# mLSTM values of all heads in 512-column projections, output gates channel-major, output projection in halves of 512

## The chip, the cores and the metric

The kernel runs on one core of a Trainium2 chip. The metric is device time in microseconds (us) for one execution: the median of 3 runs. Engines are named as in the profile: PE is TensorE (matmuls), DVE is VectorE, ACT is ScalarE, POOL is GpSimd, SP issues most of the transfers.

## The reference, cut to what matters

One block of a generator: a normalized and modulated input goes through one wide input projection into three branches (mLSTM, differential attention, state-space scan), which are merged under gates, projected, and followed by a gated conv FFN. There are 512 latent tokens and 256 context tokens, all in float32, D = 1024. The change touches the mLSTM's values `u[1]` (v) and output gates (`o_pre`), and the output projection `w_o`:

```python
u = jnp.split(h @ w_in[l], split_pts, axis=-1)          # u[0:4]: q and k, v, o gate, i and f gates of 4 heads of 128
...
def mlstm_out(h, o_pre, norm_g):
    h = rmsnorm(h.transpose(0, 2, 1, 3), norm_g.reshape(M_HEADS, M_HEAD_DIM)).reshape(bsz, t, M_WIDTH)
    return (jax.nn.sigmoid(o_pre.astype(jnp.float32)) * h).astype(o_pre.dtype)
...
def gated_merge(y_m, y_a, y_s, gate_pre, w_m, w_a, w_s, w_o):
    g_m, g_a, g_s = jnp.split(jax.nn.sigmoid(gate_pre), N_BRANCH, axis=-1)
    return (g_m * (y_m @ w_m) + g_a * (y_a @ w_a) + g_s * (y_s @ w_s)) @ w_o
...
x = x + mod[2][:, None] * gated_merge(...)              # then the second norm and the FFN
```

## The kernel before, in words

Every large product is made of three matmuls on split operands: each float32 weight and activation is kept as a high part (`wh`, `hl0` and the like) and a low part (`wl`, `hl1`), and high x high, high x low and low x high are added up in PSUM. All matmuls of projections are issued by the helper `mm` (L82), so in the profile most of PE's time has that line. A weight piece of 512 KB (`wpiece`, L180) is loaded by SP into one of 2 buffers `wr`, rounded by ACT to `wh` (L176), and DVE, or for every third piece POOL, makes `wl` (L85).

Projections come in two forms. Channel-major (`proj_cm`, L207, and `proj_w`): the weights are stationary, the tokens move, 512 latent tokens at a time (24 matmuls of 512 columns for 128 channels). Token-major (`proj_tm`, L404): 128 tokens are stationary and 256 columns of weights (`wblk`, L194: two pieces) move, 24 matmuls of 256 columns for each token tile. The values of the mLSTM are token-major, for two heads at a time and 6 token tiles (2 of context, 4 latent); so are the output gates of two heads (4 latent tiles), and the output projection in 4 blocks of 256 columns.

The order of the program is written as generators. `run(main, n_main, fill, n_fill)` (L150) spreads the chunks of a filling generator between the chunks of a main one: `m_proj(0)` (projections for heads 0 and 1) with the gate rows; then `m_core(0)` (the recurrence of those heads, small matmuls with much work on DVE and ACT between) filled with `m_proj(1)`; then `m_core(1)` filled with the first projections of the state-space branch (`s_proj(0)`), and so on. The framework then schedules this program: it sets the order on each engine once, by its own costs, and that order is fixed at run time. PSUM has 8 banks: 4 for projections (`pl`, handed out in turn by `psl`) and 4 for everything short-lived (`psx`, by `pss`). A projection can start only when the bank's earlier tile has been read by ACT and DVE. Convolution taps of q, k and of the state-space inputs read their bank once on ACT and twice on DVE (`conv_b`, L478, three taps).

The names that the prediction uses: `kw` are scaled keys, from the keys that are transposed and copied at L660 and L661; `to_cm` (L468) transposes a head's result (L472) and splits it to high and low; `xn` is the input of the second norm, transposed at L1128; the gate rows are a chain of small operations on DVE, ACT and POOL that makes the input and forget gates, ending in a matmul at 64x384.

Of the kernel before, what the change touches and what calls it, by code (L numbers as in the profile page):

```python
# [38 lines left out]
def build(tc, a, out):  # L39
# [13 lines left out]
    def open_ps(nps, nsc):  # L53
        """the pool of short-lived PSUM banks: nps single ones and nsc double ones"""
        if ps_pool:
            ps_pool.pop().close()
        st = ExitStack()
        ps_pool.append(st)
        st.tl = st.enter_context(pool("ps", nps, PSUM)) if nps else None
        st.sc = st.enter_context(pool("sc", nsc, PSUM)) if nsc else None  # L60
# [3 lines left out]
    # banks of one tag are handed out in program order, so a filling stream can have its own  # L64
# [59 lines left out]
    def rstd(o, ssq, n, inv):  # L124
        """1 / sqrt(ssq * inv + EPS) by Newton steps from an exponent-halving start"""
        rsn[0] += 1
        tg = "rs%d" % (rsn[0] % 3)
        x = cst.tile([P, 80], F32, tag=tg, name=tg, bufs=1)
        x, t = x[:, 0:n], x[:, 40:40 + n]
        ts(V, x, ssq, inv, EPS, ALU.mult, ALU.add)  # L130
        ts(V, o.bitcast(I32), x.bitcast(I32), -0.5, 1597463007.0, ALU.mult, ALU.add)
        ts(V, x, x, -0.5)
        for _ in range(3):
            tt(V, t, x, o, ALU.mult)
            tt(V, t, t, o, ALU.mult)
            stt(o, t, 1.5, o, ALU.add, ALU.mult)
# [6 lines left out]
    ssq2 = cst.tile([P, 4, 4], F32, name="ssq2")  # L143
# [6 lines left out]
    def run(main, n_main=1, fill=(), n_fill=0, hp=0, lanes=False):  # L150
        """emit main, with the chunks of fill spread evenly between its chunks"""
# [28 lines left out]
    def wpiece(w, k0, nk, c0, nc_):  # L180
        """rows [k0*P, (k0+nk)*P), columns [c0, c0+nc_) as hi and lo parts [P, nk, nc_]"""
        r = wp.tile([P, 1024], F32, tag="wr", name="wr", bufs=2).rearrange("p (k c) -> p k c", c=nc_)
        lo = wp.tile([P, 1024], F32R, tag="wl", name="wl", bufs=4).rearrange("p (k c) -> p k c", c=nc_)
        nc.sync.dma_start(r, w.rearrange("(k p) c -> p k c", p=P)[:, k0:k0 + nk, c0:c0 + nc_])
        hi = wp.tile([P, 1024], F32R, tag="wh", name="wh", bufs=4).rearrange("p (k c) -> p k c", c=nc_)
        split(hi, lo, r)
        return hi, lo
# [43 lines left out]
    def mod_bc(m, dst, mul=1.0):  # L231
        """rows m, broadcast over the partitions, times mul"""
# [7 lines left out]
    with pool("ph0", 1) as p0:  # L240
        # rows: c, c_ctx, norm1_g, norm2_g
# [68 lines left out]
        # rows of per-gate constants: bias, a_log, sign, dt row mask, ln of the key scale  # L310
# [22 lines left out]
        def h_part(n):  # L333
            """shift and scale of the channels of part n, and h there"""
# [32 lines left out]
        def early(n):  # L367
            """part n of the first projections"""
# [35 lines left out]
    def proj_tm(w, t):  # L404
# [7 lines left out]
        return pl[:, 0:256]  # L412

# [8 lines left out]
    def pcol(which, r):  # L422
        return PT[:, which, r:r + 1]
# [35 lines left out]
    def junk(n):  # L459
        return up.tile([P, 256], mybir.dt.bfloat16, tag="jk", name="jk", bufs=2)[:, 0:n]  # L460
# [7 lines left out]
    def to_cm(y, col):  # L468
        """token-major [P, 4, P] -> channel-major hi/lo [P, T], scaled by col"""
# [3 lines left out]
        hi, lo = ytile()  # L473
        act(hi, tp, AF.Identity, scale=col)
# [139 lines left out]
    def m_proj(hq, st):  # L614
        st["q"], st["k"], st["v"] = [], [], []

        def vals():
            for _ in range(2 - len(st["v"])):
                v = v3(t3(), 130)
                G.memset(v[:, :, 128:130], 1.0)  # L620
                st["v"].append(v)

        if hq == 0:
            vals()
# [15 lines left out]
        w = wblk(w_in, C_VM + hq * 256)  # L640
        vals()
        for t in range(6):
            pt = proj_tm(w, t)
            for hh in range(2):
                S.copy(st["v"][hh][:, t, 0:P], pt[:, hh * P:(hh + 1) * P])  # L645
            if t % 2:
                yield

    def m_core(hq, st, ys):
# [67 lines left out]
        w = wblk(w_in, C_OM + hq * 256)  # L717
        for j in range(4):
            so = xw()
            act(so, proj_tm(w, 2 + j), AF.Tanh, scale=0.5)  # L720
            for hh in range(2):
                ho = hb[hh][:, j, :]
                ts(V, ho, ho, sq[:, hh * 4 + j:hh * 4 + j + 1])
                stt(ho, so[:, hh * P:(hh + 1) * P], 1.0, ho, ALU.add, ALU.mult)
        for hh in range(2):
            ys.append(to_cm(hb[hh], pcol(2, R3_MN + 2 * hq + hh)))
        yield

# [162 lines left out]
    def a_keys(st):  # L891
        """keys of both heads as [hi;lo] along the contraction"""
# [19 lines left out]
    def a_core(p, st, of):  # L912
        so = sm(8)

        def queries(hh, j):
            """[hi;hi] and [lo;lo] of both sub-heads"""
# [101 lines left out]
    def weave(g_, h_, n):  # L1018
        """n chunks of h_ after each of g_"""
# [11 lines left out]
    def mods(s, rt, at, then):  # L1031
        """one modulation section for c: weighted rows summed on the way in, over the partitions at the end"""
# [35 lines left out]
    NP_M, NB_M, NP_S, NB_S, NR = 7, 15, 5, 11, 13  # L1068
    run(m_proj(0, m0), NP_M, gate_rows(), NR)
    run(m_core(0, m0, ym), NB_M, m_proj(1, m1), NP_M)  # L1070
# [63 lines left out]
    wo = {}  # L1134
    for blk, js in ((0, (0, 1, 2, 3)), (1, (0, 1, 2, 3)), (2, (0, 1)), (3, (0, 1)), (2, (2, 3)), (3, (2, 3))):
        if blk not in wo:
            wo[blk] = wblk(a["w_out"][0], blk * 256)
        w = wo[blk]
        for j in js:
            ps = pss()  # L1140
            for k in range(NK):
                hi, lo = w[k // 4]
                for n, (zt, wt) in enumerate(((zh_, hi), (zh_, lo), (zl_, hi))):
                    mm(ps[:, 0:256], zt[k][:, j * P:(j + 1) * P], wt[:, k % 4, :], k == 0 and n == 0, k == NK - 1 and n == 2)
            t_ = xw()
            xc = x1[j][blk // 2][:, (blk % 2) * 256:(blk % 2 + 1) * 256]
            tt(V, t_, ps[:, 0:256], mb[:, blk * 256:(blk + 1) * 256], ALU.mult)
            tt(V, xc, xc, t_, ALU.add)
            act(junk(256), xc, AF.Square, accum=ssq2[:, j, blk:blk + 1])
        if blk == 2 and js[0] == 2:  # L1150
            with tc.high_priority(1000):
                norm2(0, lambda: t2()[:, 0:256])
# [64 lines left out]
    for half in range(2):  # L1217
        # the last token tile is finished in column halves
# [60 lines left out]
```

## Time and profile before

| | |
|---|---|
| median of 3 runs | 1130.47 us (1129.69 to 1135.66) |
| the profiled execution: span from first to last instruction | 1133.3 us |
| mean granted clock of PE, share of full speed | 0.986 |
| PE busy | 1088.3 us, 96% |
| DVE, ACT, POOL busy | 721.9, 477.6, 285.3 us (64%, 42%, 25%) |
| chain that ended last, by engine | PE 80%, DVE 9%, DMA 3%, ACT 3%, POOL 2% |

The profiled execution is one more than the three that are timed, and the page gives its span alone. A span of 1133.3 us with 1088.3 busy on one engine leaves 45 us in which that engine did nothing. The chain that ended last is followed back from the last instruction, at each step to what released it.

### The profile page before, as it was taken

What the parts mean: (1) busy time and instruction counts of PE and PEld (TensorE: products, weight loads), DVE (VectorE), ACT (ScalarE), POOL (GpSimd) and SP (SyncE); (2) the same over time, 40 slices, a digit from 0 to 9 for tenths busy, and PEclk for the clock granted to TensorE, in tenths of its full rate; (3) what the DMA queues carried; (4) which work ended last, traced back from release to release, by engine and by line L of the source; (5) the groups of instructions that cost most, each with busy time, mean ns of one, the idle gap of its engine ahead of it and who ended that gap; (6) DMA issues with size and microseconds to landing.
All of it is one profiled execution on the core that took longest, in us unless ns stands there. A gap on an engine that the chain in (4) does not pass through costs nothing.

```text
span 1133.3 us, 16687 instructions
## 1 busy us (share of the span) xinstructions
PE 1088.3 (96%) x6438; PEld 949.7 (84%) x6438; DVE 721.9 (64%) x1354; ACT 477.6 (42%) x891; POOL 285.3 (25%) x243
## 2 busy tenths in 40 slices
PE   4998999999999998999999999988999999999998
PEld 3597999988888997889998887988888888888887
DVE  6578677768645568886685567677867656651211
ACT  5455454557324233334654573333543443431110
POOL 3230001026423533551061002243212212111110
PEclk9898999999999998999999999999999999999999
DMA  8621212223334337331113202425533333333421
GB/s 297 232 59 56 71 40 57 57 70 94 112 109 117 119 108 230 91 109 54 38 38 81 74 33 79 144 63 159 152 112 93 93 100 91 107 93 93 130 93 38
DMA packets 136416, 113.00 MB, mean 100 GB/s; under 512 B 6609, under 2 KB 115512, under 8 KB 136336
## 3 DMA queue, kind: packets, MB, share of 16 engines
q1 hardware_dynamic: 135712, 111.59, 32.8%
q8 instruction: 51, 0.84, 0.3%
q0 software_dynamic: 624, 0.33, 0.2%
q14 instruction: 29, 0.24, 0.1%
HBM read 109.81 MB, written 2.10 MB: 99 GB/s over the span
## 4 chain that ended last, share of the span: by engine, by line
PE 80%; DVE 9%; DMA 3%; issue 3%; ACT 3%; POOL 2%; SPq 0%; DVEq 0%; ACTq 0%; POOLq 0%
PE pl L82 56%; PE psx L82 19%; DVE t L85 2%; PE sc L82 2%; DMA wr<-in_w_in_dram 1%; ACT t L104 1%; DVE wl L85 1%; DVE t L88 1%; DMA wm<-in_w_mod_dram 1%; PE pl L949 1%; POOL t L85 1%; ACT wh L176 1%; POOL wl L85 1%; DMA t<-in_w_mod_dram 0%; PE psx L276 0%
## 5 line engine op out<-in xcount | busy, mean ns | idle before, releaser
L85 POOL TENSOR_TENSOR wl<-wr,wh 128x1024 fp32r<-128x1024 f32 x59 | 144.5, 2450 | 629.9 <-ACT wh L176 563.4
L176 ACT CAST wh<-wr 128x1024 fp32r<-128x1024 f32 x150 | 157.9, 1053 | 292.9 <-PE pl L82 179.5
L82 PE MATMUL pl<-h,wh 128*128 128x512 f32 (+1 forms) x768 | 223.2, 375 | 4.5 <-DVE ft L88 3.0
L85 DVE TENSOR_TENSOR wl<-wr,wh 128x1024 fp32r<-128x1024 f32 x91 | 119.2, 1312 | 146.8 <-ACT wh L176 144.6
L82 PE MATMUL pl<-hl,wh 128*128 128x512 f32 x608 | 200.4, 397 | 0.6 <-ACT t L758 0.4
L82 PEld LDWEIGHTS pl<-h,wh 128*128 128x128 f32 x768 | 141.0, 189 | 31.0 <-issue 4.1
L82 PE MATMUL pl<-wh,hl 128*128 128x256 f32 x768 | 151.7, 291 | 3.2 <-ACT t L645 3.2
L82 PE MATMUL pl<-h,wl 128*128 128x512 f32 (+1 forms) x384 | 143.0, 374 | 0.0
L82 PEld LDWEIGHTS pl<-hl,wh 128*128 128x128 f32 x608 | 113.0, 189 | 24.5 <-issue 2.0
L82 PEld LDWEIGHTS pl<-wh,hl 128*128 128x128 f32 x768 | 125.2, 196 | 4.1 <-ACT t L645 3.4
L82 PE MATMUL pl<-hl,wl 128*128 128x512 f32 x304 | 120.7, 397 | 0.0
L82 PE MATMUL pl<-wl,hl 128*128 128x256 f32 x384 | 111.3, 290 | 0.0
L82 PEld LDWEIGHTS pl<-h,wl 128*128 128x128 f32 x384 | 72.6, 189 | 12.8
L82 PEld LDWEIGHTS pl<-wl,hl 128*128 128x128 f32 x384 | 75.2, 196 | 0.5
L88 DVE SCALAR_TENSOR_TENSOR ft<-pl,PT,ft 128x511 f32<-128x511 f32 x88 | 65.2, 744 | 6.1 <-ACT ft L104 4.8
L82 PEld LDWEIGHTS pl<-hl,wl 128*128 128x128 f32 x304 | 57.3, 188 | 11.4
L82 PE MATMUL psx<-wl,ah 128*128 128x512 f32 (+1 forms) x176 | 66.2, 376 | 0.0
L82 PE MATMUL psx<-wh,al 128*128 128x512 f32 (+1 forms) x176 | 66.1, 376 | 0.0
L82 PE MATMUL psx<-wh,ah 128*128 128x512 f32 (+1 forms) x176 | 66.0, 376 | 0.0
L85 DVE TENSOR_TENSOR al<-ft,ah 128x512 fp32r<-128x512 f32 x22 | 45.4, 2063 | 31.0 <-ACT ah L176 31.0
L82 PE MATMUL pl<-y,wh 128*128 128x512 f32 x192 | 61.8, 402 | 0.4 <-ACT y L104 0.3
L104 ACT ACTIVATE t<-t 128x512 f32<-128x512 f32 (+4 forms) x55 | 36.9, 684 | 35.7 <-DVE t L88 34.2
(315 smaller groups left out, 2032.2 us busy)
## 6 DMA issues: line engine op xcount, KB each, us to landing
wr<-in_w_in_dram SPq DMA_DIRECT2D x64, 512.0 KB, 4.1
wr<-in_w_up_dram SPq DMA_DIRECT2D x44, 512.0 KB, 3.8
t<-in_w_mod_dram SPq DMA_DIRECT2D x48, 256.0 KB, 4.3
wr<-in_w_down_dram SPq DMA_DIRECT2D x22, 512.0 KB, 3.7
wm<-in_w_mod_dram SPq DMA_DIRECT2D x16, 512.0 KB, 8.1
wr<-in_w_out_dram SPq DMA_DIRECT2D x8, 512.0 KB, 3.4
fc<-in_w_mod_dram SPq DMA_DIRECT2D x16, 256.0 KB, 3.0
xs<-in_x_dram SPq DMA_DIRECT2D x2, 1024.0 KB
```

The costliest lines, as they stand in the source:

```text
L82: return PE.matmul(o, l, r, start=start, stop=stop)
L85: eng.tensor_tensor(out=o, in0=x, in1=y, op=op)
L88: V.scalar_tensor_tensor(out=o, in0=x, scalar=sc, in1=y, op0=op0, op1=op1)
L104: return S.activation(o, x, f, **kw)
L176: S.copy(hi, src)
L949: PE.transpose(out=tp[:, t * P:(t + 1) * P], in_=p0[:, (t0 + t) * P:(t0 + t + 1) * P], identity=ident)
```

## The change

**Values.** `tm_wide` projects the values of all four heads in one go, in `m_proj(0)`. It holds 4 pieces of 2 k-blocks x 512 columns, opens three token tiles at once, each a whole bank of 512 columns, and runs the pieces as the outer loop: 144 matmuls of 512 columns in place of 288 of 256. The values go to four buffers of the `y` tag, which are free until the first branch is finished, and no longer to `t3` tiles; four memsets for their last two columns stand at the beginning. `m_proj(1)` has only q and k of its two heads left, so that the filling of `m_core(0)` is 4 chunks, and `m_proj(0)` counts 12.

**Gates.** In `m_core` the output gates of each head are projected channel-major, 24 matmuls of 512 columns, and the product with (gate + 1) moves behind the transposes, into `to_cm`, where DVE reads the transposed result from PSUM. The scaling of the rows becomes one operation of 128x512 for each head.

**Output projection.** Two halves of 512 columns with pieces of 2 k-blocks; half 0 takes all four token tiles at once, with the pieces as the outer loop; half 1 takes tiles 0 and 1, then 2 and 3. 192 matmuls of 512 in place of 384 of 256. The second norm of tiles 0 and 1 is emitted after the second piece of the last group.

```diff
+    def tm_wide(c0, tiles, sink, n=3):
+        ws = [wpiece(w_in, 2 * i, 2, c0, 512) for i in range(4)]
+        for g0 in range(0, len(tiles), n):
+            grp = [(t, psl()) for t in tiles[g0:g0 + n]]
+            for i, (hi, lo) in enumerate(ws):
+                for t, pl in grp:
...
+                    for kk in range(2):
+                        k = 2 * i + kk
+                        for m, (wt, v) in enumerate(((hi, 0), (lo, 0), (hi, 1))):
+                            mm(pl, h_[v][:, k, tsl], wt[:, kk, :], k == 0 and m == 0, k == NK - 1 and m == 2)
+                    if i == 3:
+                        sink(t, pl)
+                yield
...
-    def to_cm(y, col):
+    def to_cm(y, col, gate=None):
...
         hi, lo = ytile()
+        if gate is not None:
+            stt(gate, gate, 1.0, tp, ALU.add, ALU.mult)
+            tp = gate
         act(hi, tp, AF.Identity, scale=col)
...
+    mv = [v3(ybuf().bitcast(F32), 130, 780) for _ in range(4)]
...
-        w = wblk(w_in, C_VM + hq * 256)
-        vals()
-        for t in range(6):
-            pt = proj_tm(w, t)
-            for hh in range(2):
-                S.copy(st["v"][hh][:, t, 0:P], pt[:, hh * P:(hh + 1) * P])
-            if t % 2:
-                yield
+        else:
+            def sink(t, pl):
+                for h in range(4):
+                    S.copy(mv[h][:, t, 0:P], pl[:, h * P:(h + 1) * P])
+
+            yield from tm_wide(C_VM, range(6), sink)
...
         rstd(sq, sq, 8, 1.0 / P)
-        w = wblk(w_in, C_OM + hq * 256)
-        for j in range(4):
-            so = xw()
-            act(so, proj_tm(w, 2 + j), AF.Tanh, scale=0.5)
-            for hh in range(2):
-                ho = hb[hh][:, j, :]
-                ts(V, ho, ho, sq[:, hh * 4 + j:hh * 4 + j + 1])
-                stt(ho, so[:, hh * P:(hh + 1) * P], 1.0, ho, ALU.add, ALU.mult)
+        so = []
         for hh in range(2):
-            ys.append(to_cm(hb[hh], pcol(2, R3_MN + 2 * hq + hh)))
+            pl, _ = proj_cm(wcol(C_OM + (2 * hq + hh) * P))
+            so.append(t2())
+            act(so[hh], pl, AF.Tanh, scale=0.5)
+            tt(V, hb[hh], hb[hh], sq[:, hh * 4:hh * 4 + 4].unsqueeze(2).broadcast_to([P, 4, P]), ALU.mult)
+        for hh in range(2):
+            ys.append(to_cm(hb[hh], pcol(2, R3_MN + 2 * hq + hh), so[hh]))
...
-    NP_M, NB_M, NP_S, NB_S, NR = 7, 15, 5, 11, 13
+    NP_M, NB_M, NP_S, NB_S, NR = 12, 15, 5, 11, 13
-    run(m_core(0, m0, ym), NB_M, m_proj(1, m1), NP_M)
+    run(m_core(0, m0, ym), NB_M, m_proj(1, m1), 4)
...
-    for blk, js in ((0, (0, 1, 2, 3)), (1, (0, 1, 2, 3)), (2, (0, 1)), (3, (0, 1)), (2, (2, 3)), (3, (2, 3))):
...
+    for half in range(2):
+        ws = [wpiece(a["w_out"][0], 2 * i, 2, half * 512, 512) for i in range(4)]
+        for js in (((0, 1, 2, 3),), ((0, 1), (2, 3)))[half]:
+            grp = [(j, pss()) for j in js]
+            for i, (hi, lo) in enumerate(ws):
+                for j, ps in grp:
+                    for kk in range(2):
...
+                            mm(ps, zt[k][:, j * P:(j + 1) * P], wt[:, kk, :], k == 0 and n == 0, k == NK - 1 and n == 2)
+                if js == (2, 3) and i == 1:
+                    with tc.high_priority(1000):
+                        norm2(0, lambda: t2()[:, 0:256])
```

The order on ACT at the value projection of `m_proj(0)`, before; `pl_803` and `pl_830` are the banks of the first two value tiles, `pl_717` and `pl_718` those of the keys of head 1, and `t_702` is the logarithm of the gate rows:

```order
L645 COPY t_662<-pl_803 128x128 [waits PE_49]
L645 COPY t_664<-pl_803 128x128
L104 ACT_TABLE_LOAD [waits DVE_49]
L104 ACTIVATE t_702<-t_671 64x768 [waits Activation_49]
L104 ACTIVATE t_767<-pl_718,PT 128x256
L104 ACTIVATE t_767<-pl_717,PT 128x512
L645 COPY t_662<-pl_830 128x128 [waits PE_49]
L645 COPY t_664<-pl_830 128x128
```

The same place in the order of the change; `pl_712` and `pl_713` are the keys' banks, `pl_796` and `pl_797` the first two value tiles, `t_769` the logarithm:

```order
L104 ACTIVATE t_762<-pl_713,PT 128x256 [waits PE_49]
L104 ACTIVATE t_762<-pl_712,PT 128x512
L104 ACT_TABLE_LOAD
L104 ACTIVATE t_769<-t_675 64x768 [waits DVE_49]
L659 COPY y<-pl_796 128x128 [waits PE_49]
L659 COPY y<-pl_796 128x128 x3
L659 COPY y<-pl_797 128x128 [waits PE_49]
L659 COPY y<-pl_797 128x128 x3
```

The taps of the keys have moved ahead of the table load and the logarithm, and each value tile has four copies in place of two.

The order on PE at the turn from the first mLSTM core to the second, before; the transposes at L660 are those of the next head's keys, `pl_1915` the last tile of the first X projection of the state-space branch, `pl_2048` and `pl_2049` the second:

```order
L660 MATMUL psx<-ident,t_1188 128x128 [waits PE_49]
L660 MATMUL psx<-ident,t_1188 128x128
L82 MATMUL pl_1915<-hct,wh 128x256
L82 MATMUL pl_1914<-hl_104,wl 128x512
L82 MATMUL pl_1915<-hct,wl 128x256
L82 MATMUL pl_2048<-hl_104,wh 128x512 [waits Activation_49]
L82 MATMUL pl_2049<-hct,wh 128x256 [waits Activation_49]
L82 MATMUL pl_2048<-hl_105,wh 128x512
L82 MATMUL pl_2049<-hct,wh 128x256
```

The same place in the change; L489 are the transposes in `to_cm`, L674 those of the keys, `kw` the first matmuls of the next core, and `pl_1984` the third projection of the state-space branch:

```order
L489 MATMUL psx<-ident,t_1036 128x128 [waits DVE_49,PE_49]
L489 MATMUL psx<-ident,t_1036 128x128 x3
L674 MATMUL psx<-ident,t_1234 128x128 x4
L674 MATMUL psx<-ident,t_1234 128x128 [waits PE_49]
L674 MATMUL psx<-ident,t_1234 128x128
L82 MATMUL psx<-y,kw 128x130 [waits DVE_49,PE_49] x2
L82 MATMUL psx<-y,kw 128x130 [waits DVE_49,Activation_49]
L82 MATMUL psx<-y,kw 128x130 [waits DVE_49]
L82 MATMUL psx<-y,kw 128x130 [waits DVE_49,Activation_49]
L82 MATMUL pl_1984<-hct,wh 128x256 [waits DVE_49]
```

Both X projections, which stood on both sides of the turn, now stand ahead of it; between the transposes and `pl_1984` only the `kw` matmuls are left.

## Rows read from the trace of the kernel before

**Rows 1.** the page's table: engine, busy us (share of the span), instructions
```profile
PE 1088.3 (96%) x6438; PEld 949.7 (84%) x6438; DVE 721.9 (64%) x1354; ACT 477.6 (42%) x891; POOL 285.3 (25%) x243
```

**Rows 2.** windows of PE: start:end, length, busy (matmuls), granted clock, DMA share, GB/s
```profile
380.00:390.00 10.00, 10.00 (x85) 1.00 0.00 0
715.00:735.00 20.00, 20.00 (x172) 1.00 0.35 96
850.00:900.00 50.00, 50.00 (x222) 1.00 0.33 95
```

**Rows 3.** chain that ended last, 80 to 112 us: start, length, what
```profile
85.44 1.28 ACT L104
86.73 0.84 ACT t L104
87.60 1.23 ACT t L104 x2
88.83 0.33 ACT t L645 x2
89.21 19.18 PE pl L82 x109
```

**Rows 4.** timeline of DVE: start, length, line, operation, out<-in, count [idle before]
```profile
102.92 2.35 DVE L85 TENSOR_TENSOR wl<-wr,wh 128x1024 fp32r<-128x1024 f32 x2
105.19 0.55 DVE L85 TENSOR_TENSOR t<-ident,sm 64x384 f32<-64x384 f32 x1
```

**Rows 5.** timeline of PE, the first matmul behind the gate rows' chain
```profile
108.32 0.91 PE L82 MATMUL psx<-t,on 64*128 64x384 f32 x2
```

**Rows 6.** windows of PE: stretches with waits, and what follows them
```profile
85.00:89.00 4.00, 1.04 (x9) 0.88 0.38 111
89.00:95.00 6.00, 5.79 (x27) 0.51 0.01 3
593.00:596.00 3.00, 0.81 (x8) 1.00 0.00 0
596.00:600.00 4.00, 4.00 (x23) 0.58 0.00 0
672.00:675.00 3.00, 1.99 (x17) 1.00 0.01 3
750.00:758.00 8.00, 4.95 (x37) 1.00 0.46 131
```

**Rows 7.** all waits of PE in 108:262, for what: us, times, longest
```profile
PE pl L82 <- DVE t L88: 0.5, 1, 0.5
```

**Rows 8.** timeline of PE at the turn to the second mLSTM core
```profile
183.69 0.60 PE L660 MATMUL psx<-ident,t 128*128 128x128 f32 x4
189.46 1.06 PE L82 MATMUL psx<-t,kw 128*128 128x130 f32 x8
```

**Rows 9.** timeline of ACT at the same turn
```profile
183.78 1.27 ACT L104 ACTIVATE y<-psx,PT 128x512 fp32r<-128x512 f32 x2 [3.05 <-PE psx L472]
184.94 0.86 ACT L661 COPY t<-psx 128x512 f32<-128x512 f32 x2
```

**Rows 10.** timeline of DVE at the same turn
```profile
184.50 1.41 DVE L88 SCALAR_TENSOR_TENSOR y<-psx,PT,y 128x512 fp32r<-128x512 f32 x2 [2.97 <-ACT y L104]
185.83 0.87 DVE L92 TENSOR_SCALAR kw<-t,t 128x128 f32<-128x128 f32 x4
187.92 2.18 DVE L88 SCALAR_TENSOR_TENSOR t<-pl,PT,t 128x511 f32<-128x511 f32 x4
```

**Rows 11.** waits of PE in 695:765, around the output projection
```profile
PE pl L1128 <- DVE xn L92: 1.4, 1, 1.4
PE pl L82 <- DVE t L94: 1.2, 1, 1.2
PE psx L82 <- POOL t L85: 1.0, 2, 0.5
PE psx L82 <- DVE t L85: 0.8, 1, 0.8
PE pl L1128 <- DVE t L94: 0.4, 1, 0.4
```

More of the change, by code (lines that the diff above doesn't have):

```diff
@@ L142, in build @@
     PT = cst.tile([P, 3, P], F32, name="PT")
-    ssq2 = cst.tile([P, 4, 4], F32, name="ssq2")
+    ssq2 = cst.tile([P, 4, 2], F32, name="ssq2")
     rsq2 = cst.tile([P, 4], F32, name="rsq2")
@@ L412, in proj_tm @@
         return pl[:, 0:256]
+    def tm_wide(c0, tiles, sink, n=3):
[4 more added lines that the diff above has]
+                for t, pl in grp:
+                    h_, t0 = (hctx, t) if t < 2 else (hlat, t - 2)
+                    tsl = slice(t0 * P, (t0 + 1) * P)
+                    for kk in range(2):
[5 more added lines that the diff above has]
+                yield
     def conv3(o, u, n, w0, w1, w2, b=None):
@@ L459, in junk @@
     def junk(n):
-        return up.tile([P, 256], mybir.dt.bfloat16, tag="jk", name="jk", bufs=2)[:, 0:n]
+        return up.tile([P, 512], mybir.dt.bfloat16, tag="jk", name="jk", bufs=2)[:, 0:n]
     def sm(n):
@@ L611, in conv_all @@
         conv_b(o[:, TC:NT], pl, T, wrow, brow, ci)
+    mv = [v3(ybuf().bitcast(F32), 130, 780) for _ in range(4)]
+    for v in mv:
+        G.memset(v[:, :, 128:130], 1.0)
     def m_proj(hq, st):
[L615 to L623, printed above, removed]
-            vals()
+        st["q"], st["k"] = [], []
+        st["v"] = mv[2 * hq:2 * hq + 2]
         for hh in range(2):
@@ L639, in m_proj @@
                 act(x, x, AF.Silu)
-        w = wblk(w_in, C_VM + hq * 256)
-        vals()
-        for t in range(6):
-            pt = proj_tm(w, t)
-            for hh in range(2):
-                S.copy(st["v"][hh][:, t, 0:P], pt[:, hh * P:(hh + 1) * P])
-            if t % 2:
-                yield
+        else:
[3 more added lines that the diff above has]
+            yield from tm_wide(C_VM, range(6), sink)
     def m_core(hq, st, ys):
@@ L1132, in norm2 @@
             tt(G if k % 2 else V, h2l[:, k, hs], t_, h2h[:, k, hs].bitcast(F32), ALU.subtract)
-    wo = {}
-    for blk, js in ((0, (0, 1, 2, 3)), (1, (0, 1, 2, 3)), (2, (0, 1)), (3, (0, 1)), (2, (2, 3)), (3, (2, 3))):
[L1136 to L1152, printed above, removed]
+    for half in range(2):
+        cs = slice(half * 512, (half + 1) * 512)
+        ws = [wpiece(a["w_out"][0], 2 * i, 2, half * 512, 512) for i in range(4)]
[4 more added lines that the diff above has]
+                    for kk in range(2):
+                        k = 2 * i + kk
+                        for n, (zt, wt) in enumerate(((zh_, hi), (zh_, lo), (zl_, hi))):
+                            mm(ps, zt[k][:, j * P:(j + 1) * P], wt[:, kk, :], k == 0 and n == 0, k == NK - 1 and n == 2)
+                if js == (2, 3) and i == 1:
+                    with tc.high_priority(1000):
+                        norm2(0, lambda: t2()[:, 0:256])
+            for j, ps in grp:
+                t_ = t2()
+                xc = x1[j][half]
+                tt(V, t_, ps, mb[:, cs], ALU.mult)
+                tt(V, xc, xc, t_, ALU.add)
+                act(junk(512), xc, AF.Square, accum=ssq2[:, j, half:half + 1])
     br.close()
```

## The prediction, as it was put on record

> **What bounds the kernel now.** I read the page's table of busy time first: TensorE (PE) is busy 96% of a 1133.3 us span [rows 1]. So a change pays only where it shortens PE's own stream or closes one of the gaps in the missing 4%, and it costs wherever it opens a new gap. Next I listed PE's waits by stretch. Between 108 and 262 us, which is both mLSTM cores, PE waits once, for 0.5 us [rows 7]: that stretch is full, with nothing to win and much to lose. Around the change there are two places with gaps: one wait of 3.2 us inside the first value projection, which I followed in the chain of waits [rows 3], and several of 0.3 to 1.4 us around the output projection [rows 11]. Everything below is a difference laid on the median of the runs, 1130.47 us; the profiled execution's span lies 2.8 us (0.25%) above that and within the runs' own spread. Half a per cent, 5.65 us, is about what a measurement of this kernel can tell from no change.
>
> **Term 1, wider matmuls.** 864 matmuls of 256 columns become 432 of 512: 288 for 144 in the values, 192 for 96 in the gates, 384 for 192 in the output projection. A stretch of pure 256-column work issues 85 in 10 us, 117.6 ns each; the output projection itself 172 in 20 us, 116.3 ns; pure 512-column work 222 in 50 us, 225.2 ns [rows 2]. A pair of 256 for one of 512 saves 2 x 117.6 - 225.2 = 10.0 ns, or 7.4 ns by the output projection's row. 432 times that is 4.3 us, at least 3.2; I take 4.3 and allow 5.4, as much the other way. The Trainium skill, "TensorE: Matmul & The Clock Gate", section "Wait — 56ns, not 53.3ns?", puts the fixed cost of a warm matmul at about 2.5 ns; by that estimate this term is 432 x 2.5 = 1.1 us. The rows show about 11 ns over 256 columns at 2.4 GHz instead, so the measurement decides.
>
> **Term 2, the wait inside the values.** Now PE stops before 89.21 us for a bank. The chain shows why: ScalarE (ACT) copies value tiles out of PSUM (L645), but ahead of these copies in its queue stand a table load, a logarithm and two convolution taps of the gate rows' chain, which start only at 85.44 us [rows 3]. PE waits 3.2 us, and after it the granted clock is 0.51, half of 2.4 GHz, for 6 us [rows 6]: 6.0 x 0.49 = 2.9 us more. After the change a value tile takes 24 x 225 = 5.4 us instead of 2.8, three tiles are open at once, and the convolution taps stand ahead of the logarithm (order on ACT in the section on the change). Going down PE's new order with these durations, no bank is asked for before ACT has emptied it, so both parts go: 6.1 us. They don't all come through. The matmul at 108.32 us [rows 5] opens the core and needs a small tile of the gate chain, ready at 105.74 (105.19 + 0.55 [rows 4]), 2.6 us early. In the new order the two weight splits ahead of that tile, 2.35 us, stand behind it, so it is ready at 103.4; PE would be there some 1.5 us sooner. So PE gains 108.32 - 103.4 = 4.9 us. Bounds 3 (the splits still in the way) and 6.1.
>
> **Term 3, the start of the output projection.** PE waits there 1.0 us in two pieces for POOL and 0.8 for VectorE (DVE), for the last parts of the merged z [rows 11]. Before, the first 24 matmuls (2.8 us) need all eight parts. After, half 0 takes the weight pieces as the outer loop: parts 0 and 1 for all four token tiles first (24 matmuls of 225 ns, 5.4 us), and parts 6 and 7 only 16.3 us after the start. The 1.8 us go; bounds 0 and 2.4 (a little is lost around each wait).
>
> **Term 4, the turn from one mLSTM core to the next.** This is the cost. Before, PE has the values of pair 1 as filling work inside the first core. After, these 72 (of 512 columns) lie ahead of it, so filling runs out sooner. The scheduler has by then pulled both X projections of the SSD ahead of the turn, which fills all four banks, and the next filler (pl_1984) must wait until VectorE has taken its second convolution tap from the bank of the first X. That tap stands behind the whole turn. From the first of the 14 transposes (0.11 us apart, 1.5 us in all [rows 8]): four transposes with their drain 0.6; the new product with the gate on DVE 0.70 (nearest row: a product of the same shape from PSUM, 1.41 for 2 [rows 10]); the cast on ACT 0.64 and the copy of the keys some 0.5 behind it [rows 9]; four kw 0.87; then on DVE three taps at 2.18 / 4 and three small ones at 0.87 / 4, 2.3 [rows 10]. Sum 5.6 us. PE has the transposes and five kw matmuls (some 0.12 each [rows 8]) to do in it, 2.1 us. Idle: 3.5 us, no single gap above 2.
>
> The same happens between the two heads of the second core, where the bank of pl_1983 is wanted for the gate projection: keys transposed and copied 1.1, kw 0.87, then four taps 2.18 and some nine small operations 2.0 on DVE, 6.2 us, against 14 transposes and seven kw matmuls, 2.3: idle 3.9. At the end of the first core the last four tiles' matmuls stand nearly back to back; two waits like that of rows 7 make 1.0. For all three nothing is the lower bound (a tap that comes earlier), 10.5 the upper (a fifth more on the two chains). The gates' own arithmetic is no term: 8 scalings and 8 products of 128x128 per pair become two products of 512 and two from PSUM, about the same DVE time, and only the latter move behind the transposes, which is in the 0.70 above.
>
> **Term 5, the clock.** PE is busy 2.1 of 5.6 and 2.3 of 6.2 us in these turns, 37%. Where it was busy 26% (85 to 89 us) or 27% (593 to 596), half clock followed; where 62% (750 to 758) or 66% (672 to 675), none did [rows 6]. 37% is nearer to the first. Yet all falls followed one long wait, and here none is above 2 us. I take one fall, at 2.5 us (between 1.7, from 4.0 us at 0.58, and 2.9); bounds none and two, 0 to 5.8.
>
> **Term 6, the second norm.** Before, transposes of xn wait 1.4 and 0.4 us and the first FFN matmul 1.2 [rows 11]. After, two groups of 10.9 us replace four blocks. The chain behind tiles 0 and 1 gets two more us of cover ahead of its first transposes, but only 2 matmuls (0.45 us) instead of 21 (2.5 us) between its transposes. I take these as equal: 0, bounds -2 and +2. Weight pieces keep their number and size in bytes; gate rows get 512 B long and value rows 2 KB, and no wait on those transfers stands in this stretch [rows 7]: 0.
>
> **Sum.** -4.3 - 4.9 - 1.8 + 1.0 + 3.5 + 3.9 + 2.5 = -0.1 us: 1130.4 us, no change.
>
> **Rivals.** (a) *The turns stay covered.* If the taps come early, terms 4 and 5 vanish and 4.3 + 4.9 + 1.8 = 11.0 us remain: 1119.5 us. For it: today's stretch waits 0.5 us in 154 [rows 7], and the scheduler places other work if there is some. Against it: the order it has chosen shows the four banks taken. It is faster by my bound as long as terms 4 and 5 are under 5.3 us. (b) *Filling is what the cores live on, and all that was moved comes back as waits.* One mechanism: the values that filled the first core, 144 x 117.6 ns = 16.9 us, no longer cover its chains on DVE and ACT. Then -11.0 + 16.9 = +5.9, with one fall of the clock +8.4: 1138.9 us. It decides from 16.7 us of new idle time and lost clock on. For it: both cores are full only through such filling; against: DVE has slack in the first, and later filling is pulled forward. (c) *The change does only its first term*: the wait of term 2 moves to another bank, the turns cost little: -4.3 to -2, 1127 us; inside the forecast's band.
>
> **Chances.** The forecast with (c): 0.46, between 1125 and 1136. Rival (a), also with half of the idle time: 0.25. Rival (b): 0.29. The range reaches to both rivals: down to (a), 1119.5, and up past (b) to 1141, with a tenth left out on each side. Faster by over 0.5%: 0.25; within: 0.46; slower: 0.29.
>
> **What would show it.** Term 1: 512-column stretches at 225 ns in place of 256 at 117.6. Term 2: no wait for ACT inside the values and the core's first matmul near 103.4 plus what order moves. Term 3: no POOL wait at the output projection's start. Terms 4 and 5: PE waits for DVE at the transposes, kw matmuls, and the first matmuls of pl_1984 and pl_2257, 3 to 4 us in each turn, with half clock behind one. I am wrong if PE's waits in the two cores stay near 0.5 us, or if waits appear all through them, not only at the turns.

## The result, and the profile after

The changed kernel takes 1142.87 us (median of 4 runs, 1142.25 to 1143.97) against 1130.08 for the kernel before (4 runs, 1127.85 to 1135.66): a ratio of 1.0107, 95% interval 1.0084 to 1.013. It is slower by 1.1%, above the predicted range of 1119.5 to 1141. The spans of the two profiles differ by 7.7 us only, the medians by 12.8: in the later runs of the kernel before, the device time is 1.7 to 1.9 us above the span, so that its profiled execution (span 1133.3) would stand at some 1135 us (an estimate), near the slowest of its runs. Another profile of the kernel before (e4 below) has a span of 1130.1 and the same waits.

The page of the kernel after:

```profile
span 1141.0 us, 15756 instructions
PE 1088.0 (95%) x6006; PEld 930.6 (82%) x6006; DVE 709.8 (62%) x1314; ACT 474.8 (42%) x871; POOL 285.1 (25%) x243
```

PE has 432 matmuls less and is busy as long as before [rows 1]: what the wider ones save comes back as matmuls at half clock (mean granted clock 0.984 in place of 0.986), and the longer span is waits. Windows of PE in the kernel after (start:end, length, busy (matmuls), granted clock, DMA share, GB/s):

```profile
83.00:100.00 17.00, 17.00 (x77) 1.00 0.11 31
187.00:190.00 3.00, 0.47 (x5) 1.00 0.00 0
190.00:193.00 3.00, 2.80 (x12) 0.53 0.69 180
219.00:222.40 3.40, 0.40 (x4) 1.00 0.16 16
226.00:230.00 4.00, 3.76 (x15) 0.50 0.01 3
...
180.00:262.00 82.00, 74.00 (x406) 0.94 0.15 41
```

The values (83 to 100 us) now run without a gap at 17.00 / 77 = 221 ns a matmul, and the gap and half clock of [rows 6] at 85 us are gone. In return PE is busy 74.00 of 82 us from 180 on; the same window of the kernel before, in a fence of its own, held 81.46 (the same by the clock: the cores begin some 6 us later there):

```profile
180.00:262.00 82.00, 81.46 (x538) 1.00 0.22 59
```

PE's waits in the kernel after, in 100:262 and then in 695:800 (for what: us, times, longest):

```profile
PE psx L82 <- DVE kw L92: 6.5, 4, 3.0
PE psx L82 <- DVE t L85: 2.3, 4, 0.8
PE pl L82 <- ACT t L104: 1.2, 2, 0.8
...
PE pl L82 <- DVE ft L88: 4.7, 1, 4.7
PE pl L82 <- DVE t L94: 2.2, 1, 2.2
PE pl L1140 <- DVE t L94: 1.6, 2, 1.1
```

Where the cores waited 0.5 us in all [rows 7] they now wait 10.2 (with a wait of 0.2 that is not shown). At the output projection the waits for `t L85` of [rows 11] are gone, those around the norm (`L1140` and `t L94`) are 3.8 instead of 3.0, and the FFN's wait for `ft` is 4.7 us. The PE timeline of the kernel after, at the start of the first core and at the two turns:

```profile
101.94 0.91 PE L82 MATMUL psx<-t,on 64*128 64x384 f32 x2 [0.79 <-DVE t L85]
...
185.78 1.04 PE L489 MATMUL psx<-ident,t 128*128 128x128 f32 x8
186.66 0.82 PE L674 MATMUL psx<-ident,t 128*128 128x128 f32 x6
190.05 2.38 PE L82 MATMUL psx<-y,kw 128*128 128x130 f32 x10 [2.58 <-DVE kw L92]
...
218.59 0.82 PE L674 MATMUL psx<-ident,t 128*128 128x128 f32 x6
222.40 1.19 PE L82 MATMUL psx<-y,kw 128*128 128x130 f32 x8 [3.00 <-DVE kw L92]
```

and what DVE and POOL do meanwhile:

```profile
186.42 1.28 DVE L88 SCALAR_TENSOR_TENSOR t<-t,psx 128x512 f32<-128x512 f32 x2 [2.83 <-PE psx L489]
187.90 1.81 DVE L88 SCALAR_TENSOR_TENSOR y<-t,PT,y 128x512 fp32r<-128x512 f32 x1 [0.19 <-ACT y L104]
189.63 0.86 DVE L92 TENSOR_SCALAR kw<-t,t 128x128 f32<-128x128 f32 x4
...
218.42 2.34 DVE L88 SCALAR_TENSOR_TENSOR sm<-t 128x2 f32<-128x2 f32 x1
```

```profile
186.81 2.35 POOL L85 TENSOR_TENSOR wl<-wr,wh 128x1024 fp32r<-128x1024 f32 x1 [28.50 <-ACT wh L176]
218.40 2.35 POOL L85 TENSOR_TENSOR wl<-wr,wh 128x1024 fp32r<-128x1024 f32 x1 [29.23 <-ACT wh L176]
```

At each turn PE has the 14 or 6 transposes and then nothing until the first `kw`: single waits of 2.58 and 3.00 us, and a granted clock of 0.53 and 0.50 behind them. Both chains on DVE are stretched: while POOL makes a `wl`, a product of 128x512 takes 1.81 us and one on 128x2 takes 2.34, where the same operations elsewhere take 0.7 ([rows 10]: 1.41 for two) and some 0.15.

### The profile page after: what moved, and what is told of

The parts are those of the page before. It is cut to its first block, busy times and chain, and to the rows that moved or that the text cites. A ratio compares the mean times of both kernels' runs of the same rounds, so it can differ in the third digit from the quotient of the medians.

```text
span 1141.0 us, 15756 instructions
## 1 busy us (share of the span) xinstructions
PE 1088.0 (95%) x6006; PEld 930.6 (82%) x6006; DVE 709.8 (62%) x1314; ACT 474.8 (42%) x871; POOL 285.1 (25%) x243
## 4 chain that ended last, share of the span: by engine, by line
PE 80%; DVE 9%; DMA 4%; issue 3%; ACT 3%; POOL 1%; SPq 0%; DVEq 0%; POOLq 0%; ACTq 0%
PE pl L82 58%; PE psx L82 17%; DVE t L88 2%; PE sc L82 2%; DVE t L85 2%; DMA t<-in_w_mod_dram 1%; POOL wl L85 1%; ACT wh L176 1%; ACT t L104 1%; DMA wm<-in_w_mod_dram 1%; PE pl L961 1%; DVE t L560 1%; DMA fc<-in_w_mod_dram 1%; DMA xs<-in_ctx_dram 1%; PE psx L276 1%
## 5 line engine op out<-in xcount | busy, mean ns | idle before, releaser
L85 POOL TENSOR_TENSOR wl<-wr,wh 128x1024 fp32r<-128x1024 f32 x59 | 143.4, 2431 | 613.2 <-ACT wh L176 584.4
L82 PE MATMUL pl<-hl,wh 128*128 128x512 f32 x672 | 221.2, 400 | 1.5 <-ACT t L104 1.2
L85 DVE TENSOR_TENSOR wl<-wr,wh 128x1024 fp32r<-128x1024 f32 x91 | 116.9, 1286 | 168.9 <-ACT wh L176 166.8
L82 PEld LDWEIGHTS pl<-hl,wh 128*128 128x128 f32 x672 | 125.4, 190 | 28.5 <-issue 2.0
L82 PE MATMUL pl<-hl,wl 128*128 128x512 f32 x336 | 133.2, 396 | 0.0
L82 PE MATMUL pl<-wh,hl 128*128 128x256 f32 (+1 forms) x576 | 119.0, 299 | 0.0
L82 PEld LDWEIGHTS pl<-wh,hl 128*128 128x128 f32 x576 | 94.0, 192 | 3.1
L82 PE MATMUL pl<-wl,hl 128*128 128x256 f32 (+1 forms) x288 | 85.9, 298 | 0.0
L82 PEld LDWEIGHTS pl<-hl,wl 128*128 128x128 f32 x336 | 63.7, 190 | 12.8
L85 DVE TENSOR_TENSOR al<-ft,ah 128x512 fp32r<-128x512 f32 x22 | 46.8, 2126 | 30.9 <-ACT ah L176 30.9
L82 PEld LDWEIGHTS pl<-wl,hl 128*128 128x128 f32 x288 | 55.4, 192 | 2.2 <-issue 0.5
```

Source lines behind the costliest of these rows:

```text
L82: return PE.matmul(o, l, r, start=start, stop=stop)
L85: eng.tensor_tensor(out=o, in0=x, in1=y, op=op)
```

## The experiments

Ratios are to the kernel before on the same chip, whose medians were 1131.50, 1130.59, 1131.62 and 1131.63 us in the four groups (e1 to e4, e5 to e8, e9 to e12, e13 to e15).

**The three parts alone.** e1 is the kernel before with `tm_wide` and its counts (`NP_M`, the 4 chunks), e2 with the hunks of `to_cm` and `m_core`, e3 with the hunk of the output projection, each as in the diff of the change; e4 is the kernel before, unedited.

> Only the values change (512 columns, all heads in the first projection phase, output buffers); gates and output projection as before. Theory A (the filling that left the first core is what is missing at the two turns): most of the loss is here. In the stretch from the first projections to the state-space core this kernel ends 7 to 11 us later than before, with waits of PE for kw at one turn at least above 2 us and half clock behind it; in all 1136 to 1141 us. Theory B (the gates' product behind the transposes is what lengthens the turns): the values alone gain their 1.4 us of wider matmuls and the 5 us of the wait inside them: 1123 to 1127 us.

Measured: 1131.72, ratio 1.0001 (0.9984 to 1.0018). The wait at 85 us is gone, and a new one of 2.1 us stands at the first turn (PE timeline, and windows of PE behind it):

```profile
184.12 0.70 PE L489 MATMUL psx<-ident,t 128*128 128x128 f32 x2 [2.08 <-DVE t L88]
```

```profile
182.00:186.00 4.00, 1.83 (x15) 1.00 0.00 0
186.00:190.00 4.00, 4.00 (x37) 1.00 0.00 0
```

From 180 on the kernel before has PE busy 81.46 us, and e1 has

```profile
180.00:262.00 82.00, 77.59 (x514) 1.00 0.20 54
```

The time lies between the theories: the values gain what terms 1 and 2 say, and lose most of it again in the cores, 3.9 us in this window, at full clock. Alone they are not the cause of the 1.1%.

> Only the gates change (channel-major, product behind the transposes). Theory A: the filling of the first core is still there, so the turns stay short: 1128 to 1132 us, 1 us less from 96 pairs of wider matmuls. Theory B: 1135 to 1140 us, with waits of PE for kw of 1.5 to 3 us at the turn from the first core to the second.

Measured: 1138.56, ratio 1.0063 (1.004 to 1.0087): the largest loss of the three. Waits of PE in 100:262:

```profile
PE psx L82 <- DVE kw L92: 2.8, 3, 1.9
PE pl L82 <- ACT t L104: 0.8, 1, 0.8
```

The time is theory B's, the place is not: the first turn is untouched, and the second has the wait for `kw` of the full change, with half clock behind it (0.67 in 224:228). From 180 on:

```profile
180.00:262.00 82.00, 77.87 (x448) 0.98 0.19 50
```

> Only the output projection changes. By the two traces the stretch from its start to the first FFN matmul shrinks by 2.4 us, and the second norm behind it gives up to 3 us back: both theories 1127 to 1131 us. A time of 1134 or more would say that the output projection is part of the loss.

Measured: 1134.72, ratio 1.0032 (1.0015 to 1.005). The gain of term 3 is there (no wait at the start), and more is lost at the end. Waits of PE in 695:800, then the window behind the norm:

```profile
PE pl L82 <- DVE ft L88: 5.1, 1, 5.1
PE pl L82 <- DVE t L94: 2.0, 1, 2.0
PE pl L1128 <- DVE t L94: 1.6, 2, 1.2
```

```profile
753.00:757.00 4.00, 3.94 (x18) 0.50 0.49 135
```

DVE in e3, ahead of the tap that the FFN's first product waits for:

```profile
776.80 5.91 DVE L88 SCALAR_TENSOR_TENSOR fc<-fc,scl 128x512 f32<-128x512 f32 x5 [2.80 <-DMA fc<-in_b_mod_dram]
782.63 0.74 DVE L88 SCALAR_TENSOR_TENSOR ft<-pl,PT,ft 128x511 f32<-128x511 f32 x1
```

> The kernel before, unchanged, profiled once more: the profile shown so far has a span of 1133.3 us, above the median of the runs. Expected: a span of 1126 to 1130 us, and the place where the 3 to 7 us of difference lie, in the stretches outside the change (start, waits for modulation weights) by theory A and B alike.

Measured: one run, 1131.85, with the waits of [rows 7, 11], and `ft` at 2.5 us. DVE at the place of the last fence:

```profile
774.83 5.29 DVE L88 SCALAR_TENSOR_TENSOR fc<-fc,scl 128x512 f32<-128x512 f32 x4 [2.28 <-DMA fc<-in_b_mod_dram]
780.04 0.74 DVE L88 SCALAR_TENSOR_TENSOR ft<-pl,PT,ft 128x511 f32<-128x511 f32 x1
```

The order on DVE has one operation more ahead of the tap in e3, and the row of them starts 2 us later, when a transfer has landed; both push the tap. The three parts sum to 0.0 + 0.63 + 0.32 = 0.95%, near the 1.07% of the whole: they lose separately, mostly.

**What in the output projection costs.** e5 does half 0 as in the change, ahead of the loop over the blocks of 256 columns, which is that of before without its first two blocks:

```diff
-    for blk, js in ((0, (0, 1, 2, 3)), (1, (0, 1, 2, 3)), (2, (0, 1)), (3, (0, 1)), (2, (2, 3)), (3, (2, 3))):
+    for blk, js in ((2, (0, 1)), (3, (0, 1)), (2, (2, 3)), (3, (2, 3))):
```

> Output projection alone, first half in 512 columns with the pieces outside, second half in blocks of 256 in the order of before. Theory C (what the output projection loses comes from its last groups of 512: only 2 matmuls are left behind the first transposes of the second norm, and everything behind it, up to the FFN's modulation sums on DVE, comes later): the 1.8 us of waits at its start go, some 1 us of wider matmuls is gained, the norm waits 3.0 us as before and the wait for the modulation sums stays at 2.5 us: 1127 to 1129.5 us. Rival (the wide pieces themselves, their transfers or their banks, cost it): 1132 or more, like the full change of the output projection.

Measured: 1129.12, ratio 0.999 (0.9972 to 1.0008). Waits of PE in 695:800:

```profile
PE pl L82 <- DVE ft L88: 3.4, 1, 3.4
PE pl L1128 <- DVE xn L92: 1.4, 1, 1.4
PE pl L82 <- DVE t L94: 1.2, 1, 1.2
PE pl L1128 <- DVE t L94: 0.4, 1, 0.4
```

The start's waits stay away and those of the norm are again [rows 11]. So the last two groups of 512 are what costs: 0.32 + 0.10 = 0.42%, 4.7 us (the two intervals together leave 2 to 7.5). The profiles agree: from the first matmul of the output projection to the FFN's first product it takes 84.3 us in e3 and 79.7 in e5. The groups differ in their loops too (pieces outside, two tiles at once), so width is not taken apart from order.

**What in the gates costs: POOL, the place, the filling.** e6 is e2 with the split at the turn on DVE instead of POOL:

```diff
-        tt(G if sp[0] % 3 == 0 else V, lo, src, hi.bitcast(F32), ALU.subtract)
+        tt(G if sp[0] % 3 == 0 and sp[0] != 24 else V, lo, src, hi.bitcast(F32), ALU.subtract)
```

> Gates alone, and one weight split (the 24th of the program, the one that POOL makes at 217.9 us of the run with the gates alone) moved from POOL to DVE, where a gap of 1.5 us stands in its order. Theory D (POOL's split runs beside DVE's small operations there and stretches one from 0.3 to 1.2 us; that and the half clock behind it are the loss): the wait for kw falls from 1.9 to about 1 us, no half clock, 1132 to 1135 us. Rival (the missing filling at the turn between the heads of the second core is all of it): the wait for kw stays above 1.5 us and the time at 1137 to 1139.

Measured: 1136.45, ratio 1.0062 (1.0038 to 1.0085). Waits of PE in 212:226, and windows:

```profile
PE psx L82 <- DVE kw L92: 1.8, 2, 1.2
```

```profile
212.00:220.00 8.00, 6.68 (x41) 1.00 0.40 95
220.00:226.00 6.00, 5.22 (x18) 0.50 0.14 44
...
180.00:262.00 82.00, 78.82 (x449) 0.96 0.19 51
```

The single wait fell from 1.9 to 1.2 us, the time did not: neither theory. In this profile PE idles 1 us less from 180 on than in e2, and loses 3.2 us to the clock in place of 1.6. The split now stands on DVE right ahead of the same chain. So the stretch beside POOL is real, and e6 does not show what the kernel would take without it.

e8 is e2 with the two gate projections issued ahead of the last output loop of the core (`if hh:` before `for j in range(4)`, products where they were).

> Gates alone, with both gate projections written ahead of the last output loop of each core instead of behind it. If the gates lose because their tile asks for a bank late, behind the convolution taps, the waits between 200 and 260 us (7 us more than before) go and the time is 1130 to 1132 us. If filling at the turn between the heads decides, taking these projections out of the end moves the waits to the end of the core, and the time stays at 1136 to 1140 us.

Measured: 1136.08, ratio 1.0053 (1.0036 to 1.007), with a wait for `kw` of 2.9 us. An earlier place does not help.

e7 (on e1) and e10 (on e2) add filling to the second core, the first X projection of the next state-space group; e9 does so in the full change:

```diff
-    run(m_core(1, m1, ym), NB_M, s_proj(0, s0), NP_S - 1)
+    sp1 = s_proj(1, s1)
+    run(m_core(1, m1, ym), NB_M, chain(s_proj(0, s0), take(sp1, 1)), NP_S)
...
-        weave(chain(s_proj(1, s1), merge(0, "w_branch_m", ym, True)), mods(2, t2, t2, to_row), 1), 32 + NP_S, 1000)
+        weave(chain(sp1, merge(0, "w_branch_m", ym, True)), mods(2, t2, t2, to_row), 1), 32 + NP_S, 1000)
```

> Values alone, and one more projection of the state-space branch (the first X of its second group) given to the second mLSTM core as filling. If missing filling is what the values cost, the waits of 6.7 us between 180 and 260 us in the run with the values alone shrink by half or more: 1127 to 1129 us. If they come from the order around the first turn alone (transposes waiting 2.1 us for DVE at 182 us), nothing changes there: 1131 to 1133 us, and the state-space core may wait more.

Measured: 1129.08, ratio 0.9989 (0.9973 to 1.0005). The time is that of missing filling, but it is 0.12% under e1's with intervals that overlap, and the waits don't bear it out: 4.6 us in 100:262 after 5.2 in e1, the 2.1 at the first turn among them.

> Gates alone with the same additional filling. Theory E: 1130 to 1132 us, the wait for kw under 1 us and no half clock behind it. Rival: 1136 to 1139 us.

Measured: 1134.85, ratio 1.0023 (1.0006 to 1.004), between the two. The wait for `kw` is gone, 0.4% of the gates' 0.63 come back, and a new wait of 2.0 us stands at 244 us.

> The whole change, with one more projection (the first X of the second state-space group) as filling of the second mLSTM core; in its order a gate projection stands between the kw matmuls at the turn between the heads, where the change has none. Theory E (at that turn the change has nothing left to put between: that and the half clock behind it are the gates' loss): the 7 us of waits and clock between 216 and 232 us shrink to 2 or less and the time falls by 5 to 7 us, to 1135 to 1138 us. Rival (the loss only moves on, to the state-space core that has this work less): 1141 to 1143 us.

Measured: 1145.31, ratio 1.012 (1.0096 to 1.0145): nothing comes back, and it is above the rival too. Waits of PE in 100:262:

```profile
PE psx L82 <- DVE kw L92: 2.6, 1, 2.6
PE pl L82 <- ACT t L104: 2.4, 2, 2.0
```

The second turn is filled, the first (2.6 us) is as it was, and further waits stand behind. Too little filling in the second core is not the whole of it.

**Parts together.** e11 is e7 with the output projection of e5; e12 is e9 with it.

> A version that keeps what gained: values in 512 columns with the additional filling, output projection with only its first half in 512, gates as before. From the single runs (values with filling 0.9989, first half 0.999): 1127 to 1129 us, faster than both kernels; if the two share a gain, 1129 to 1131.

Measured: 1127.24, ratio 0.9959 (0.9943 to 0.9975), faster than both kernels.

> The whole change with the additional filling and the second half of the output projection in blocks of 256 as before. Theory C and E together: 4 to 5 us under the full change with filling, 1130 to 1133 us. If the output projection's tail is no cause of its own, the same as the full change with filling.

Measured: 1138.89, ratio 1.0059 (1.0036 to 1.0081), above the 1130 to 1133 expected, since theory E's part did not come. Against e9 the output's last groups are worth 0.61%; against e11 the gates cost 1.0%, with the filling in both.

**The width of the gates' tiles.** e13 (on e2), e14 (on e12) and e15 (on the full change) keep the gates channel-major and the product behind the transposes, and narrow the tiles to 256 tokens:

```diff
-            pl, _ = proj_cm(wcol(C_OM + (2 * hq + hh) * P))
+            hi, lo = wcol(C_OM + (2 * hq + hh) * P)
             so.append(t2())
-            act(so[hh], pl, AF.Tanh, scale=0.5)
+            for c in (slice(0, 256), slice(256, 512)):
+                pl = psl()
+                for k in range(NK):
+                    for n, (wt, v) in enumerate(((hi, 0), (hi, 1), (lo, 0))):
+                        mm(pl[:, 0:256], wt[:, k, :], hlat[v][:, k, c], k == 0 and n == 0, k == NK - 1 and n == 2)
+                act(so[hh][:, c], pl[:, 0:256], AF.Tanh, scale=0.5)
```

> The kernel before with the gates channel-major and the product behind the transposes, as in the change, but the projection in four tiles of 256 tokens instead of two of 512 for a pair of heads (192 matmuls of 256 columns again). Theory F (the gates lose because two wide tiles leave nothing to place between the keys' transposes and the kw matmuls at the turn of the second core; in this kernel's order 20 matmuls of 256 stand there): no wait for kw above 0.5 us in 210 to 225, the clock stays at 1.00 there, and the time is that of before within 0.2%: 1129 to 1133. Theory G (the loss comes from the product's new place, in the chain behind the transposes, whatever the tile size): still 1135 to 1139, with the waits at L489 and behind it.

Measured: 1134.61, ratio 1.0029 (1.0008 to 1.0051), between the theories: no wait for `kw` is left, but PE waits 2.3 us in the middle of the next stretch, at 228 us, for a state that DVE adds up.

> Wide values, gates channel-major in 256, the first X projection of the second state-space group as filling, half 0 of the output projection wide and half 1 in blocks: e12 with the gates' tiles narrowed. Theory F: the turn inside the second core is covered, and what is left is the turn between the cores (a wait of about 2.6 us and its half clock): 4 to 7 us below e12's 1138.9, so 1132 to 1135. Theory G: as e12, 1137 to 1140.

Measured: 1127.55, ratio 0.9968 (0.9949 to 0.9986): 0.9% below e12, more than theory F gave, since the first turn is free of waits too. The largest group of PE's waits in 100:262:

```profile
PE psx L82 <- DVE t L85: 3.3, 4, 1.2
```

> The full change with nothing but the gates' tiles narrowed to 256 tokens. In its order no matmul stands between the keys' transposes and the first kw at the turn of the second core, since the filling of that core is spent earlier. Theory F says that a narrow tile helps only where the order puts it into the turn: the wait of about 3 us for kw stays, and the time is 1140 to 1144, at most 1.1 us worse for the narrower matmuls. If narrow tiles help wherever they stand (theory H, shorter bank holds): 1134 to 1138.

Measured: 1136.73, ratio 1.0032 (1.0014 to 1.005): theory H's number. F's mechanism is at work all the same, at the turn where I had not looked. PE at the first turn, the window of PE from 180 on, and POOL's splits in 170:235:

```profile
180.61 0.82 PE L674 MATMUL psx<-ident,t 128*128 128x128 f32 x6
...
186.25 1.06 PE L82 MATMUL psx<-y,kw 128*128 128x130 f32 x8
```

```profile
180.00:262.00 82.00, 77.09 (x508) 1.00 0.22 57
```

```profile
189.92 2.38 POOL L85 TENSOR_TENSOR wl<-wr,wh 128x1024 fp32r<-128x1024 f32 x1 [30.66 <-ACT wh L176]
225.74 2.35 POOL L85 TENSOR_TENSOR wl<-wr,wh 128x1024 fp32r<-128x1024 f32 x1 [32.93 <-ACT wh L176]
```

Between the transposes and `kw` the order now has 29 matmuls of an X projection, by their count the second (14 of 512 and 15 of 256 columns, 4.9 us), and in the full change none: there both X projections stand ahead of the turn. PE does not wait in 180:190, and no half clock follows. At the second turn nothing stands in between, as I had read, and PE waits 0.8 and 0.6 us instead of 3.0. POOL's splits have moved away from DVE's chain at both turns, which the edit did not set out to do.

## Why the prediction was wrong

**Terms 1 to 3 hold in direction.** The values run at 221 ns a matmul where two of 256 took 235 [rows 2]: 14 ns a pair there, and 10 at the 225 ns of the long 512 stretch, as the term has it. Over the whole kernel the saving is rather 2 to 3 us than 4.3: PE's busy time times its granted clock goes from 1088.3 x 0.986 to 1088.0 x 0.984 (an estimate; the rounding of the clock alone is worth half a us on either side). The Trainium skill's fixed cost of 2.5 ns ("TensorE: Matmul & The Clock Gate", section "Wait — 56ns, not 53.3ns?") does not agree with the rows of the long stretches, which lie 11 to 12 ns above their columns at 2.4 GHz. Term 2 forecast the first core at 103.4; it starts at 101.94, with 0.79 us of wait left. Not all of the 6.4 us to [rows 5] are the change's: the same matmul stands at 104.14 to 108.52 us in the nine profiles without the wide values (mean 106.9) and at 101.76 to 103.79 in the eight with them (mean 102.6), 4.3 us where the term has 4.9. Term 3's waits are gone in the full change, e3 and e5.

**Terms 4 and 5: the places were right, the waits nearly right by luck, the clock too low.** The working gave 8.4 us of waits (1.0 at the end of the first core, 3.5 and 3.9 at the turns) and 2.5 of clock, "no single gap above 2". The full change shows 1.7 us at the end of the first core (174 to 177 us) and 6.5 for `kw` at the turns, in gaps up to 2.58 and 3.00; with the smaller ones, 10.2 us of waits against 0.5. Term 5 took one fall of the clock and two came: in 180:262 a clock of 0.94 on 74.00 us, 4.4 us. Together 14.1 in place of 10.9.

That the turns came near 7.4 is luck, since two errors in the working stand against each other. The stretch of DVE's operations beside POOL's split was not in the sum: 1.1 us at the first turn (0.7 to 1.81) and 2.2 at the second (0.15 to 2.34). And the chains were priced too long: without the stretch, 6.5 - 3.3 = 3.2 us of waits are left at the two turns (an estimate; e15, whose second turn is bare too but has no stretch, waits 1.4 there). At the second turn it also counted 14 transposes for PE where there are 6, and the upper bound has a slip: a fifth more on the two chains makes 10.8, not 10.5.

The cause was laid on the wrong part, or on the smaller one: on the filling that went with the values. e1, which moves them alone, has PE idle 3.9 us more from 180 on and no half clock, and terms 1 and 2 give that back. e2, with the gates alone, has 3.6 us more and 1.6 of clock; the full change 7.5 and 4.4. So the idle time of the parts adds up and the half clock does not: the first turn stands bare only where both are done (the change, e9, e12). The gates as a source of idle time were in the prediction only as "about the same DVE time". e13 to e15 show that the width of their tiles decides over most of it: narrowed, with all else kept, they give back 0.75% in the full change (1.0107 to 1.0032), 0.9% in e14, and in e13 0.34 of 0.63, where the intervals still touch.

What width does can be followed in the order and the trace: the 24 matmuls of a tile of 512 take 5.4 us and hold their bank at least as long, those of 256 take 2.8 [rows 2]; with two wide tiles the scheduler put both X projections ahead of the first turn, with four smaller ones it kept one for the turn. Why its costs lead it there was not tried. Nor is this filling taken apart from POOL's splits, which left both turns in the same three runs. By the durations in e15, the 4.9 us of matmuls cover the first turn's gap with or without the stretch, and at the second turn, where nothing stands between, the single wait is shorter by 2.2 us, which is the stretch that has gone.

**Term 6 is the step that failed outright.** It was taken as 0, bounds -2 and +2. e3 against e5 gives 4.7 us for the last two groups of 512, e9 against e12 0.61%, 6.9 us. Some 2.6 us of the 4.7 are the term's own subject: with only two matmuls between the transposes of the norm, the waits are 3.6 us in e3 where e5 has 3.0, and of the two half clock follows them in e3 alone (3.94 us at 0.50 in 753:757, 2.0 us); it does so in the profiles of the full change, e9 and e15 too. The other 2 us lay outside what I costed: DVE's row of `fc` products has one operation more and starts later, behind a transfer, and the FFN's first product waits 5.1 us instead of 3.4 (2.5 to 3.4 in the profiles that end in blocks of 256). This division is read from the two traces, not from a run of its own, and why the transfer lands later was not followed.

**The sum.** With what was measured for each term it is -2.5 - 4.3 - 1.8 + 8.9 + 4.4 + 4.7 = +9.4 us (8.9 are the 10.2 us of waits less the 0.5 of before and the 0.8 that term 2's measure holds already), or +11.6 with the 6.9 of e9 and e12; the ratio says 12.1 (9.5 to 14.7). So term 6 is the largest miss, then the clock and term 1, some 2 us each. By runs: e14 is the change without the wide gates and the last groups, plus one chunk of filling, and from its 0.9968 to the full change it is 1.39%. The gates' 0.75% (e15) and the last groups' 0.42% (e5), each measured for itself, make 1.17.

Rival (a)'s 1119.5 needed the turns covered; with the first one covered and the last groups narrow, e14 stands at 1127.55. Rival (b) had nearly the right time, 1138.9, by a mechanism that the runs bear out in small part: moving the values cost e1 3.9 us in the cores where (b) has 16.9, and e9's added filling brought nothing. The waits in e2 and e13 at 228 to 267 us, behind the turn, were not taken apart.

## What to carry to other kernels

A wider matmul saves some 10 ns, but a wider tile is also a larger unit for whatever order fills the gaps: here two units of filling work in place of four, with all that their order moved, cost eight to ten times what the width saved (8.5 to 10 us against 1), so read in the order what stands between a chain's two ends before and after, at every such place and not only where you expect the wait. Here the last groups of a phase, whose results nothing else covers, lost by being wide; try them narrow (e5) and widen the rest. And measure each part alone: one part of this change was neutral, one lost by its last step only, and the version without the two losses (e11, e14) is faster than both kernels.

## What the runs showed of the hardware

A wait did not always bring the clock down. In e1, 2.08 us of wait with PE busy 1.83 of 4 us left the granted clock at 1.00; 2.58 us in the kernel after with 0.47 of 3 brought it to 0.53; and in e6 waits of 1.2 and 0.6 us, at 217 and 220 us, with busy 6.68 of 8 us in 212:220, were followed by 0.50. The length of the single wait does not tell which. Nor does it tell how long the half clock lasts: the wait of 3.2 us inside the values stands in the kernel before and, not edited, in e5, and in 82:100 the mean granted clock is 0.81 on 14.83 us of matmuls in the one and 0.91 on 14.82 in the other. So a us or so of clock between two single profiles need not come from an edit.

A DVE operation on 128x2 elements, with both tensors in SBUF, took 2.34 us, some 15 times its usual 0.15, in the time of a POOL subtraction of 128x1024 (218.42 to 220.76 and 218.40 to 220.75); at the first turn a product of 128x512 with both tensors in SBUF took 1.81 and ended 0.55 us after POOL's, while the products `t<-t,psx` of 186.42 to 187.70, with one tensor in PSUM, ran beside the same POOL operation at 1.28 for two. The Trainium skill, "SBUF — State Buffer", section "Who interferes with whom", says that a DVE instruction with two SBUF inputs contends with a GpSimd instruction that reads SBUF, that the port pair which they share is an exclusive lock, and that one with at most one SBUF input, outside the 2-port modes, does not contend. The three rows agree. One tensor in SBUF is not safe in every operation, though: in e2 a TENSOR_SCALAR that scales `kw` by a column took 1.24 us beside POOL's split (at 219.08), and 0.28 elsewhere. The change made the stretch at the first turn possible: the operation of 1.81 us read one tensor from PSUM before (`y<-psx,PT,y` [rows 10]) and reads both from SBUF now (`y<-t,PT,y`).
